# Scan steps dealt by work and tied behind a unit's matmuls, and a final norm whose sums start early

## The chip, the cores and the metric

The kernel runs on one core of a Trainium2 chip, in one launch. The metric is the device time in microseconds, median of several runs. Five instruction streams work side by side: TensorE (PE; its weight loads are PEld), VectorE (DVE), ScalarE (ACT), GpSimd (POOL) and SyncE (SP, which issues all DMAs here). Each executes its own list in order; they wait for one another through semaphores.

## The reference

One inference step of a hybrid decoder layer on 336 tokens (16 meta tokens, 256 of a prompt, 8 samples of 8). Cut to what matters here:

```python
h = rms_norm(x, norm_w)
proj = h @ w_in
z, xbc, dt_raw, sc_b, sc_c, sc_h, sc_z, g_a, g_b = split_proj(proj)
xbc_c, conv_new = causal_dwconv(xbc, conv_prev, ssd_conv_w)
xbc = jax.nn.silu(xbc_c + ssd_conv_b)
xs, bm, cm = jnp.split(xbc, [D_INNER, D_INNER + SSD_GROUPS * SSD_STATE], axis=-1)
# ssd_chunked(...), for each of 8 groups:
decay = jnp.exp(jnp.where(causal, seg, -jnp.inf))
wts = cb[..., None] * decay * dtc[:, :, None]
y_diag = jnp.einsum('bcijgr,bcjgrp->bcigrp', wts, xc)
chunk_states = jnp.einsum('bcjgr,bcjgrp,bcjgn->bcgrpn', to_end, xc, bc)
# y = y_diag + y_off; then a gated, grouped RMSNorm and a projection to D_MODEL,
# y_b = W_b(B * conv3(C * h) * silu(z_b)),
# sigmoid(g_a) * y_a + sigmoid(g_b) * y_b, the output projection, the residual, a last RMSNorm
```

## The kernel before

Channels lie on the partitions (2048 = 16 tiles of 128), tokens in the free dimension. Every product of fp32 numbers is made of three products of fp32r halves. `wblk` (L80) loads a block of 128x1024 weights (wraw, one SP DMA of 512 KB), ScalarE rounds it to whi (L84, the "hi split"), VectorE takes the rest, wlo (L86, the "lo split"). `mm` (L89) then runs 24 matmuls for a block: hi weights on hi and lo inputs (L92, L93), lo weights on hi inputs (L96). A `unit` is two such blocks into one PSUM bank "pj", of which there are two; one block of 24 matmuls is the clock of everything below. Other PSUM products use the two "ms" banks, or "yb", a tile of four banks.

First come the short conv branch and the projections around it, then eight groups of the recurrence (SSD). In group g TensorE runs four z units, then, from g = 1, the eight one-block units of `out_units(g-1)` that add the previous group's projection into ya (L646 takes two banks for each block), in groups 0 and 7 four gate units, and for g < 7 the six conv units of the next group, whose last results are BT, CT and four tiles xs: ScalarE's L394 begins a conv tile, VectorE's L396 adds the taps, L400 and L401 write xs. Between the units the 23 `yield`s of the generator `ssd(g)`, the *steps*, are dealt by `weave`. Steps named below: `rows(c)` transposes xs (L460) and BT (L462) of chunk c into two "ms" banks and multiplies BT by CT (L463); `decay(c)` is eight subtractions (L478) and an exponential (L480), for c = 1 after E = exp(W) (L476), which waits for W's broadcast load from ac_d; `state(c)` is the product L498 into an "ms" bank, copied out by L502 for c = 0; `weights(c)` multiplies (L484, L486); the samples' states are updated by L612 in two halves of two operations each, and stored (ssms). L616 and L619 spread the group norm's reciprocal root, by a diagonal and a product with ones.

The deal is by units: after unit i of n, steps run until 23 (i+1) / n are done, rounded up. The framework's scheduler then sets the order of each engine's instructions by priority and readiness in a model of time; a step may move among the splits and evacuations of the units near it.

After group 7 `out_units(7)` runs, with `merge` for the first eight tiles of ya: it loads a branch tile (mb_d) into a buffer of the tag "h0", which also holds the samples' states, and L666 and L667 write ya. The final projection has 16 units: L715 adds the residual, L717 squares, GpSimd's L719 sums the squares into sacc. The last norm (`rstd`, L114 to L125) sums over partitions by products with ones (L114, six: two tiles by three pieces of the tokens), takes the power on GpSimd (L119), and spreads the result by three diagonals (L124) and three products (L125). Sixteen scalings follow, twelve on VectorE (L729), four on ScalarE and GpSimd (L727, with the copy rsb, L735), and the stores to yT, two single tiles (L731) and seven pairs (L733).

## Time and profile before

| | us |
|---|---|
| median of three runs | 1877.46 |
| the three runs | 1880.71, 1876.68, 1877.46 |
| profiled execution | 1878.88 |
| its span | 1877.1 |
| TensorE busy | 1838.0 (98%) |
| VectorE, ScalarE, GpSimd busy | 1150.7, 752.0, 312.1 |
| mean granted TensorE clock | 0.993 of full |

A row of the timeline gives the start of an operation, its duration, engine and line, the tiles written and read, and in brackets the idle time of its engine before it with what ended that. Matmuls are pipelined, so their durations overlap and a busy TensorE isn't TensorE at its peak; a stretch is measured by its ends. The granted clock has two levels here, full (2.4 GHz) and half (1.2 GHz).

### The profile page before, as it was taken

The numbers are of one execution on the slowest core, as the hardware profiler recorded it, in microseconds if no ns is written. First come the engines' busy times: TensorE is split into PE (matmuls) and PEld (weight loads), VectorE is DVE, ScalarE is ACT, GpSimd is POOL, SyncE is SP. The second block draws the span as 40 slices with busy tenths as digits, with TensorE's granted clock in tenths as the row PEclk, the third lists the DMA queues.
The fourth block names the chain that finished last, engine by engine and source line by source line (L and its number), as shares of the span: only waits on it lengthen the run. The fifth ranks groups of instructions, "written<-read, shape, count | busy, mean of one in ns | idle before, by whom it ended". The sixth has DMA issues, their size and how long they took to land.

```text
span 1877.1 us, 31447 instructions
## 1 busy us (share of the span) xinstructions
PE 1838.0 (98%) x12622; PEld 1798.4 (96%) x12622; DVE 1150.7 (61%) x1743; ACT 752.0 (40%) x1043; POOL 312.1 (17%) x397
## 2 busy tenths in 40 slices
PE   7999999999999999999999999999999999999996
PEld 7999999999999999999999999999999999999996
DVE  6844444444534337568686776868768687674533
ACT  5433333333333335444453443534435344333432
POOL 0100000000000002131321323223232231300011
PEclk9999999999999999999999999999999999999998
DMA  6444444444444446457475564655656466575553
GB/s 219 141 153 146 147 154 149 147 148 155 150 159 156 157 159 224 154 179 241 150 235 170 184 227 157 225 170 186 217 158 228 165 200 212 169 261 169 173 171 107
DMA packets 117170, 331.74 MB, mean 177 GB/s; under 512 B 12448, under 2 KB 38688, under 8 KB 117024
## 3 DMA queue, kind: packets, MB, share of 16 engines
q1 hardware_dynamic: 117024, 329.73, 53.4%
q8 instruction: 99, 1.62, 0.3%
q14 instruction: 47, 0.39, 0.1%
HBM read 296.80 MB, written 32.88 MB: 176 GB/s over the span
## 4 chain that ended last, share of the span: by engine, by line
PE 62%; DVE 3%; DMA 2%; issue 1%; ACT 1%; POOL 0%; DVEq 0%; SPq 0%; ACTq 0%
PE pj L92 19%; PE pj L93 19%; PE pj L96 19%; PE yb L554 2%; PE ms L498 1%; DMA W<-ac_d 1%; PE ms L537 1%; DMA wraw<-w 1%; DVE cacc L396 1%; PE ms L460 1%; DVE wlo L86 1%; DVE W L478 1%; PE yb L609 0%; DVE h L612 0%; DVE ya L729 0%
## 5 line engine op out<-in xcount | busy, mean ns | idle before, releaser
L92 PE MATMUL pj<-hhi,whi 128*128 128x320 f32 (+3 forms) x2944 | 888.5, 313 | 0.0
L93 PE MATMUL pj<-hlo,whi 128*128 128x320 f32 (+3 forms) x2944 | 883.3, 312 | 0.0
L86 DVE TENSOR_TENSOR wlo<-wraw,whi 128x1024 fp32r<-128x1024 f32 x480 | 601.1, 1253 | 446.3 <-PE pj L96 283.3
L84 ACT ACTIVATE whi<-wraw 128x1024 fp32r<-128x1024 f32 x480 | 508.3, 1059 | 870.7 <-PE pj L93 801.7
L92 PEld LDWEIGHTS pj<-hhi,whi 128*128 128x128 f32 x2944 | 554.7, 188 | 4.1 <-issue 3.0
L93 PEld LDWEIGHTS pj<-hlo,whi 128*128 128x128 f32 x2944 | 553.9, 188 | 0.7
L96 PE MATMUL pj<-hhi,wlo 128*128 128x320 f32 (+3 forms) x2944 | 498.3, 311 | 0.0
L96 PEld LDWEIGHTS pj<-hhi,wlo 128*128 128x128 f32 x2944 | 453.1, 188 | 0.0
L92 PE MATMUL pj<-yh,whi 128*128 128x320 f32 x512 | 157.2, 319 | 0.0
L93 PE MATMUL pj<-yl,whi 128*128 128x320 f32 x512 | 152.3, 309 | 0.0
L92 PEld LDWEIGHTS pj<-yh,whi 128*128 128x128 f32 x512 | 96.2, 188 | 7.8 <-issue 6.7
L93 PEld LDWEIGHTS pj<-yl,whi 128*128 128x128 f32 x512 | 96.2, 188 | 1.7 <-issue 1.7
L96 PE MATMUL pj<-yh,wlo 128*128 128x320 f32 x512 | 95.8, 309 | 0.0
L396 DVE SCALAR_TENSOR_TENSOR cacc<-pad,V,cacc 128x360 f32<-128x360 f32 (+1 forms) x144 | 84.7, 588 | 9.3 <-ACT cacc L394 7.2
L646 DVE TENSOR_TENSOR ya<-ya,pj 128x320 f32<-128x320 f32 x112 | 54.4, 485 | 53.7 <-PE pj L96 52.4
L506 POOL TENSOR_TENSOR h<-h,decS 128x512 f32<-128x512 f32 x64 | 72.3, 1166 | 78.7 <-PE ms L537 78.7
L195 POOL COPY SCS<-up 128x2 f32<-128x2 f32 x16 | 19.4, 1214 | 370.9 <-DVE up L189 367.9
L96 PEld LDWEIGHTS pj<-yh,wlo 128*128 128x128 f32 x512 | 80.3, 188 | 0.0
L93 PE MATMUL pj<-vlo,whi 128*128 128x320 f32 x256 | 75.5, 309 | 0.0
L92 PE MATMUL pj<-vhi,whi 128*128 128x320 f32 x256 | 75.5, 309 | 0.0
L478 DVE TENSOR_SCALAR W<-W,act 128x128 f32<-128x128 f32 (+2 forms) x192 | 66.3, 403 | 14.6 <-DMA W<-ac_d 11.4
L389 POOL COPY pad<-cs 128x24 f32<-128x24 f32 x48 | 31.6, 661 | 130.1 <-DVE cacc L396 124.7
(211 smaller groups left out, 1483.0 us busy)
## 6 DMA issues: line engine op xcount, KB each, us to landing
wraw<-w SPq DMA_DIRECT2D x352, 512.0 KB, 3.9
wraw<-wso SPq DMA_DIRECT2D x64, 512.0 KB, 3.5
wraw<-wsc SPq DMA_DIRECT2D x32, 512.0 KB, 3.8
h<-h0T SPq DMA_DIRECT2D x32, 512.0 KB, 5.8
ssms<-h SPq DMA_DIRECT2D x32, 512.0 KB, 4.3
wraw<-wo SPq DMA_DIRECT2D x32, 512.0 KB, 3.9
xq_d<-xe SPq DMA_DIRECT2D x16, 320.0 KB, 3.4
W<-ac_d SPq DMA_DIRECT2D x8, 576.0 KB, 5.4
```

Source lines behind the costliest of these rows:

```text
L84: nc.scalar.activation(hi[:, :n], raw[:, :n], AF.Copy)
L86: nc.vector.tensor_tensor(lo[:, :n], raw[:, :n], fb(hi[:, :n]), sub)
L92: nc.tensor.matmul(out, w, xh(k0 + k), start=first and k == 0, stop=False)
L93: nc.tensor.matmul(out, w, xl(k0 + k), start=False, stop=False)
L96: nc.tensor.matmul(out, w, xh(k0 + k), start=False, stop=last and k == nk - 1)
L195: nc.gpsimd.tensor_copy(SCS[:, j, 0, :], up[:, 256:258])
L389: nc.gpsimd.tensor_copy(smp[:, :, 0:3], cs[:, 1:9, :])
L396: nc.vector.scalar_tensor_tensor(acc[:, i0:], pad[:, i0 + k:360 + k], col(V_CW, 4 * j + k), acc[:, i0:], mult, add)
L478: nc.vector.tensor_scalar(w[:n, h, :], w[:n, h, :], act[:n, c, 8 * g + h:8 * g + h + 1], 0.0, sub, ALU.min)
L506: nc.gpsimd.tensor_tensor(split(h0[b]), split(h0[b]), bc(hv(decS[:, b, :], g), [P, 8, HP]), mult)
L554: nc.tensor.matmul(yb[q * HP:(q + 1) * HP, t, t0:t0 + n], x[:, h * HP:(h + 1) * HP], w[:, h, :], start=i == 0, stop=i == 3)
L646: nc.vector.tensor_tensor(ya[:, m, :TV], ya[:, m, :TV], pp[:, :TV], add)
```

## The change

Four things change. First, `weave` counts work: a z, gate or conv unit weighs 2, an out unit 1, and after each unit as many steps run as the share of the weight passed allows, only whole ones. Second, every instruction that a step issues on TensorE, ScalarE or VectorE gets an order (not a wait on a semaphore) behind the latest L96 matmul, hi split or lo split written before it; the names are kept in `latest`. Third, E = exp(W[1]) moves from decay(1) to the step of rows(1), ahead of the loads of the samples' states. Fourth, the end: the squares of blocks 0 to 14 are summed by three products as soon as they are there, in front of the last block's end; after the last block three products, one VectorE operation, the power, one diagonal operation of 107 x 321 and one product follow; all sixteen scalings are VectorE's, and the stores go out in ten pieces.

```diff
+    latest = {}
+
     def wblk(src, n=1024):
         raw = wp.tile([P, 1024], F32, name="wraw")
         nc.sync.dma_start(raw[:, :n], src)
         hi = wp.tile([P, 1024], F32R, name="whi")
-        nc.scalar.activation(hi[:, :n], raw[:, :n], AF.Copy)
+        latest["act"] = nc.scalar.activation(hi[:, :n], raw[:, :n], AF.Copy).ins
         lo = wp.tile([P, 1024], F32R, name="wlo")
-        nc.vector.tensor_tensor(lo[:, :n], raw[:, :n], fb(hi[:, :n]), sub)
+        latest["dve"] = nc.vector.tensor_tensor(lo[:, :n], raw[:, :n], fb(hi[:, :n]), sub).ins
         return hi, lo
 
     def mm(out, hi, lo, xh, xl, base, nk, k0, first, last):
...
             w = lo[:, base + k * P:base + k * P + P]
-            nc.tensor.matmul(out, w, xh(k0 + k), start=False, stop=last and k == nk - 1)
+            latest["pe"] = nc.tensor.matmul(out, w, xh(k0 + k), start=False, stop=last and k == nk - 1).ins
...
 
             def decay(c):
                 n, m, w = CH[c][1], NT[c], W[c]
-                if c == 1:
-                    nc.scalar.activation(E, w, AF.Exp)
                 for h in range(8):
                     nc.vector.tensor_scalar(w[:n, h, :], w[:n, h, :], act[:n, c, 8 * g + h:8 * g + h + 1], 0.0,
                                             sub, ALU.min)
...
             decay(0)
             yield
+            nc.scalar.activation(E, W[1], AF.Exp)
             rows(1)
             for u in range(4):
                 h = pb.tile([P, 2, 512], F32, name="h0", bufs=4)
...
-        def weave(units, steps, lead, n):
-            done = 0
-            for i, _ in enumerate(units):
-                if i < lead:
-                    continue
-                want = (i + 1 - lead) * NSTEP / max(n - lead, 1)
-                while done < want and next(steps, "end") != "end":
+        def weave(parts, steps):
+            total, past, done = sum(n * w for _, n, w in parts), 0, 0
+            for w in (w for units, _, w in parts for _ in units):
+                past += w
+                want = NSTEP * past / total
+                traced = nc.cur_bb.bb.instructions
+                tail = traced[-1]
+                while done + 1 <= want + 1e-6 and next(steps, "end") != "end":
                     done += 1
+                new = []
+                for ins in reversed(traced):
+                    if ins is tail:
+                        break
+                    new.append(ins)
+                for ins in new:
+                    for a in latest.values():
+                        if ins.engine == a.engine:
+                            tc.add_manual_dep(ins, a.name, mybir.DependencyInfo(mybir.DependencyClass.NoSync,
+                                                                                 mybir.DependencyReason.DATA),
+                                              reason="step")
             for _ in steps:
                 pass
 
-        from itertools import chain
         S = [{} for _ in range(NG)]
         for _ in conv_units(0, S[0]):
             pass
         for g in range(NG):
-            parts = [z_units(g, S[g])]
-            n = 4
+            parts = [(z_units(g, S[g]), 4, 2)]
             if g:
-                parts.append(out_units(g - 1, S[g - 1]))
-                n += 8
+                parts.append((out_units(g - 1, S[g - 1]), 8, 1))
             if g in (0, NG - 1):
-                parts.append(gate_units(0, 4) if g == 0 else gate_units(4, 8))
-                n += 4
+                parts.append((gate_units(0, 4) if g == 0 else gate_units(4, 8), 4, 2))
             if g < NG - 1:
-                parts.append(conv_units(g + 1, S[g + 1]))
-                n += 6
-            weave(chain(*parts), ssd(g, S[g]), 0, n)
+                parts.append((conv_units(g + 1, S[g + 1]), 6, 2))
+            weave(parts, ssd(g, S[g]))
         for mp, _ in enumerate(out_units(NG - 1, S[NG - 1])):
             if mp < 4:
                 for m in (2 * mp, 2 * mp + 1):
...
-        sacc = pc_.tile([P, TV], F32, name="sacc", bufs=1)
+        sacc, sq = (pc_.tile([P, TV + 4], F32, name=n, bufs=1) for n in ("sacc", "sql"))
+        for t in (sacc, sq):
+            nc.gpsimd.memset(t[:, TV:], 0.0)
+        pr = [ps.tile([P, 512], F32, name="ms") for _ in range(2)]
+
+        def sums(i, t):
+            for c in range(3):
+                nc.tensor.matmul(pr[i][:107, c:c + 1], t[:, 107 * c:107 * c + 107], ones[:, 0:1], start=True, stop=True)
+
+        sm, r = (pc_.tile([107, 3], F32, name=n, bufs=1) for n in ("rs_m", "rs_r"))
         for m in range(KT):
             xr = pc_.tile([P, TV], F32, name="xr")
             nc.sync.dma_start(xr, xT[:, m, META:])
             po = unit(wo[m], lambda k: hhi[:, k, :TV], lambda k: hlo[:, k, :TV], TV)
             nc.vector.scalar_tensor_tensor(ya[:, m, :TV], po, 0.5, xr, mult, add)
-            sq = pc_.tile([P, TV], F32, name="sqf") if m else sacc
-            nc.scalar.activation(sq, ya[:, m, :TV], AF.Square)
-            if 0 < m < KT - 1:
-                nc.gpsimd.tensor_tensor(sacc, sacc, sq, add)
-        rs = run(rstd(pc_, [sacc, sq], META, 1.0 / DM, EPS))
-        rsb = pc_.tile([P, TV], F32, name="rsb", bufs=1)
-        for q in range(8):
-            for m in (2 * q, 2 * q + 1):
-                if q % 3 == 2:
-                    fx = pc_.tile([P, TV], F32, name="fx", bufs=4)
-                    nc.scalar.activation(fx, ya[:, m, :TV], AF.Copy, scale=col(V_FW, m))
-                    nc.gpsimd.tensor_tensor(ya[:, m, :TV], fx, rsb, mult)
-                else:
-                    nc.vector.scalar_tensor_tensor(ya[:, m, :TV], ya[:, m, :TV], col(V_FW, m), rs, mult, mult)
-                if q == 0:
-                    nc.sync.dma_start(yT[:, m, :], ya[:, m, :TV])
-            if q:
-                nc.sync.dma_start(yT[:, 2 * q:2 * q + 2, :], ya[:, 2 * q:2 * q + 2, :TV])
+            if m < KT - 1:
+                s_ = pc_.tile([P, TV], F32, name="sqf")[:, :TV] if m else sacc[:, :TV]
+                nc.scalar.activation(s_, ya[:, m, :TV], AF.Square)
+                if m:
+                    nc.gpsimd.tensor_tensor(sacc[:, :TV], sacc[:, :TV], s_, add)
+                if m == KT - 2:
+                    sums(0, sacc)
+                    nc.vector.tensor_scalar(sm, pr[0][:107, 0:3], 1.0 / DM, EPS, mult, add)
             else:
-                nc.scalar.activation(rsb, rs, AF.Copy)
+                nc.scalar.activation(sq[:, :TV], ya[:, m, :TV], AF.Square)
+        sums(1, sq)
+        nc.vector.scalar_tensor_tensor(r, pr[1][:107, 0:3], 1.0 / DM, sm, mult, add)
+        nc.gpsimd.tensor_tensor(r, r, bc(mhalf[:107], [107, 3]), ALU.pow)
+        dg = pc_.tile([107, 3, 107], F32, name="rs_d", bufs=1)
+        nc.vector.tensor_tensor(dg, bc(ident[:107, :107].unsqueeze(1), [107, 3, 107]),
+                                bc(r.unsqueeze(2), [107, 3, 107]), mult)
+        rs = ps.tile([P, 512], F32, name="pj")
+        nc.tensor.matmul(rs[:, :321], ones[:107, :], dg.rearrange("p c t -> p (c t)"), start=True, stop=True)
+        m = 0
+        for n in (1, 1, 2, 2, 2, 2, 2, 2, 1, 1):
+            for k in range(m, m + n):
+                nc.vector.scalar_tensor_tensor(ya[:, k, :TV], ya[:, k, :TV], col(V_FW, k), rs[:, :TV], mult, mult)
+            nc.sync.dma_start(yT[:, m:m + n, :], ya[:, m:m + n, :TV])
+            m += n
```

Three places in the program's order follow, the second for two engines, with the line numbers of each kernel: those of the new one are two higher in most of the code up to L476, the same from L478 to L510, and one higher from there to `merge`. In the rows, W is the exponent or weight tile of the first two chunks, W_ with a number that of the third.

VectorE at the start of a group, before; the last conv tile's xs is the fourth line from the end:

```order
L478 TENSOR_SCALAR W<-W,act 128x144 x4
L400 SCALAR_TENSOR_TENSOR xs<-cth,cacc 128x272
L401 SCALAR_TENSOR_TENSOR xs<-cth,cacc 128x64
L478 TENSOR_SCALAR W<-W,act 128x144 x4
L86 TENSOR_TENSOR wlo<-wraw,whi 128x1024
L396 SCALAR_TENSOR_TENSOR cacc<-pad_6678,V,cacc 128x360 x3
L86 TENSOR_TENSOR wlo<-wraw,whi 128x1024
L400 SCALAR_TENSOR_TENSOR xs<-cth,cacc 128x272
L401 SCALAR_TENSOR_TENSOR xs<-cth,cacc 128x64
L86 TENSOR_TENSOR wlo<-wraw,whi 128x1024
L430 SCALAR_TENSOR_TENSOR zs<-zs,pj 128x320
```

After, the same place:

```order
L88 TENSOR_TENSOR wlo<-wraw,whi 128x1024
L398 SCALAR_TENSOR_TENSOR cacc<-pad_6678,V,cacc 128x360
L478 TENSOR_SCALAR W<-W,act 128x128 x4
L402 SCALAR_TENSOR_TENSOR xs<-cth,cacc 128x272
L403 SCALAR_TENSOR_TENSOR xs<-cth,cacc 128x64
L478 TENSOR_SCALAR W<-W,act 128x128 x4
L88 TENSOR_TENSOR wlo<-wraw,whi 128x1024
L432 SCALAR_TENSOR_TENSOR zs<-zs,pj 128x320
L88 TENSOR_TENSOR wlo<-wraw,whi 128x1024
L467 TENSOR_TENSOR xdt<-ms,dtt 128x512
L88 TENSOR_TENSOR wlo<-wraw,whi 128x1024
L432 SCALAR_TENSOR_TENSOR zs<-zs,pj 128x320
```

The subtractions behind which the conv tail stood were those of decay(1) (128x144); now those of decay(0) (128x128) stand ahead of the tail and decay(1) is behind it, past the first z units.

ScalarE at the end of a group's z units, before; L429 takes a z bank, L502 copies state(0) out:

```order
L467 ACTIVATE bt<-ms 128x128
L84 ACTIVATE whi<-wraw 128x1024 x2
L429 ACTIVATE zs<-pj 128x320
L502 ACTIVATE hst<-ms 128x512
L84 ACTIVATE whi<-wraw 128x1024
L467 ACTIVATE bt<-ms 80x128
L568 ACTIVATE bhh<-bt 80x128
```

After:

```order
L86 ACTIVATE whi<-wraw 128x1024 x2
L431 ACTIVATE zs<-pj 128x320
L86 ACTIVATE whi<-wraw 128x1024
L480 ACTIVATE W_10905<-W_10905 80x640
L502 ACTIVATE hst<-ms 128x512
L469 ACTIVATE bt<-ms 80x128
L86 ACTIVATE whi<-wraw 128x1024 x6
```

The exponential of the third chunk (80x640) now stands directly ahead of L502, where it followed later, beyond the rows shown, before.

TensorE at the first out unit of a group, before; yh and yl are inputs of out_units, L498 is state(0), L460 to L463 are rows(2):

```order
L498 MATMUL ms<-xe,bt 128x512
L92 MATMUL pj<-yh,whi 128x320
L93 MATMUL pj<-yl,whi 128x320
L92 MATMUL pj<-yh,whi 128x320
L93 MATMUL pj<-yl,whi 128x320
L92 MATMUL pj<-yh,whi 128x320
L93 MATMUL pj<-yl,whi 128x320
L92 MATMUL pj<-yh,whi 128x320
L93 MATMUL pj<-yl,whi 128x320
L96 MATMUL pj<-yh,wlo 128x320 x4
L460 MATMUL ms<-CR,xs 80x128 x4
L462 MATMUL ms<-CR,BT 80x128
```

After; L462 to L465 are rows(2):

```order
L98 MATMUL pj<-yh,wlo 128x320 x4
L498 MATMUL ms<-xe,bt 128x512
L462 MATMUL ms<-CR,xs 80x128 x4
L94 MATMUL pj<-yh,whi 128x320
L95 MATMUL pj<-yl,whi 128x320
L94 MATMUL pj<-yh,whi 128x320
L464 MATMUL ms<-CR,BT 80x128
L465 MATMUL ms<-CT,BT 80x80
L95 MATMUL pj<-yl,whi 128x320
```

The state product and the rows of chunk 2, a block's part apart before, now follow one another, and the BT transpose comes a few matmuls behind.

VectorE at the start of out_units(7), with buffer numbers, before; L612 updates the samples' states, L666 and L667 are merge:

```order
L612 TENSOR_TENSOR h0_16027<-h0_16027,yb_16746 128x1024
L612 TENSOR_TENSOR h0_16029<-h0_16029,yb_16746 128x1024
L86 TENSOR_TENSOR wlo_16869<-wraw_16865,whi_16867 128x1024
L86 TENSOR_TENSOR wlo_16915<-wraw_16911,whi_16913 128x1024
L646 TENSOR_TENSOR ya_79<-ya_79,pj_16825 128x320
L666 SCALAR_TENSOR_TENSOR zs_16853<-zs_16853,ya_79 128x320
L667 TENSOR_TENSOR ya_79<-zs_16853,h0_16855 128x320
L646 TENSOR_TENSOR ya_79<-ya_79,pj_16839 128x320
L86 TENSOR_TENSOR wlo_16961<-wraw_16957,whi_16959 128x1024
L666 SCALAR_TENSOR_TENSOR zs_16859<-zs_16859,ya_79 128x320
```

After:

```order
L613 TENSOR_TENSOR h0_16028<-h0_16028,yb_16810 128x1024
L613 TENSOR_TENSOR h0_16030<-h0_16030,yb_16810 128x1024
L647 TENSOR_TENSOR ya_79<-ya_79,pj_16825 128x320
L667 SCALAR_TENSOR_TENSOR zs_16853<-zs_16853,ya_79 128x320
L647 TENSOR_TENSOR ya_79<-ya_79,pj_16839 128x320
L668 TENSOR_TENSOR ya_79<-zs_16853,h0_16855 128x320
L667 SCALAR_TENSOR_TENSOR zs_16859<-zs_16859,ya_79 128x320
L88 TENSOR_TENSOR wlo_16961<-wraw_16957,whi_16959 128x1024
L668 TENSOR_TENSOR ya_79<-zs_16859,h0_16861 128x320
L647 TENSOR_TENSOR ya_79<-ya_79,pj_16871 128x320
L667 SCALAR_TENSOR_TENSOR zs_16899<-zs_16899,ya_79 128x320
```

The second update moved to directly ahead of the first merge, behind two more lo splits.

## Rows read from the trace of the kernel before

**Rows 1.** The page, part 1: busy time of each engine, share of the span, instructions.
```profile
PE 1838.0 (98%) x12622; PEld 1798.4 (96%) x12622; DVE 1150.7 (61%) x1743; ACT 752.0 (40%) x1043; POOL 312.1 (17%) x397
```

**Rows 2.** TensorE's waits: engine, line, releaser: us in total, times, longest.
```profile
PE ms L460 <- DVE xs L400: 13.2, 7, 3.4
```

**Rows 3.** Timeline, TensorE: start, us, line, operation [idle before, releaser].
```profile
1338.78 0.33 PE L460 MATMUL ms<-CR,xs 128*128 128x128 f32 x1 [3.40 <-DVE xs L400]
```

**Rows 4.** Windows: us; busy PE, PEld, DVE, ACT, POOL; PEclk, DMA share, GB/s.
```profile
1339.40:1343.00 3.60, 3.60 (x16) 3.60 (x15) 3.57 (x5) 0.28 (x1) 1.04 (x1) 0.53 1.01 384
...
1661.00:1679.00 18.00, 18.00 (x123) 17.75 (x121) 16.50 (x30) 5.43 (x7) 0.00 (x0) 1.00 0.85 272
1870.00:1874.00 4.00, 0.00 (x0) 0.00 (x0) 1.31 (x3) 0.00 (x0) 0.00 (x0) 0.50 1.04 363
```

**Rows 5.** Timeline, ScalarE and VectorE, around a group's start.
```profile
1094.69 1.17 ACT L476 ACTIVATE E<-W 128x1152 f32<-128x1152 f32 x1 [1.56 <-DMA W<-ac_d]
...
1100.73 1.17 ACT L480 ACTIVATE W<-W 128x1152 f32<-128x1152 f32 x1 [3.13 <-DVE W L478]
1101.81 0.67 ACT L394 ACTIVATE cacc<-pad,V 128x360 f32<-128x360 f32 x1
...
1105.42 0.44 DVE L400 SCALAR_TENSOR_TENSOR xs<-cth,cacc 128x272 f32<-128x272 f32 x1
```

**Rows 6.** Timeline, all engines, end of the program.
```profile
1852.09 0.30 PE L92 MATMUL pj<-hhi,whi 128*128 128x320 f32 x1
...
1853.49 0.88 POOL L719 TENSOR_TENSOR sacc<-sacc,sqf 128x320 f32<-128x320 f32 x1 [5.91 <-ACT sqf L717]
...
1860.47 0.36 PE L114 MATMUL ms<-CR,sqf 128*112 128x1 f32 x2 [1.04 <-ACT sqf L717]
...
1861.65 0.16 DVE L118 TENSOR_SCALAR rs_m<-ms 112x3 f32<-112x3 f32 x1 [1.79 <-PE ms L114]
...
1862.79 0.47 DVE L124 TENSOR_SCALAR rs_d<-CR,rs_r 112x112 f32<-112x112 f32 x2 [0.97 <-POOL rs_r L119]
...
1865.07 1.01 DVE L729 SCALAR_TENSOR_TENSOR ya<-ya,V,ms 128x320 f32<-128x320 f32 x2 [0.86 <-PE ms L125]
...
1866.64 4.67 DVE L729 SCALAR_TENSOR_TENSOR ya<-ya,V,ms 128x320 f32<-128x320 f32 x10 [0.56 <-ACT rsb L735]
...
1868.38 4.88 SPq L733 DMA_DIRECT2D yT<-ya  x7
```

**Rows 7.** Timeline, TensorE and ScalarE, end of group 0's z units.
```profile
781.85 1.02 PE L498 MATMUL ms<-xe,bt 128*128 128x512 f32 x2
...
782.90 0.60 ACT L502 ACTIVATE hst<-ms 128x512 f32<-128x512 f32 x1 [0.42 <-PE ms L498]
...
783.55 0.31 PE L462 MATMUL ms<-CR,BT 128*80 128x128 f32 x1
```

**Rows 8.** Groups by line and shape: count | busy us, mean ns | idle before, releaser.
```profile
L86 DVE TENSOR_TENSOR wlo<-wraw,whi 128x1024 fp32r<-128x1024 f32 x480 | 601.1, 1253 | 446.3 <-PE pj L96 283.3 <-ACT whi L84 161.9
...
L612 DVE TENSOR_TENSOR h<-h,yb 128x1024 f32<-128x1024 f32 x32 | 38.7, 1215 | 0.0
...
L478 DVE TENSOR_SCALAR W<-W,act 80x80 f32<-80x80 f32 x64 | 22.2, 406 | 0.5 <-DMA W<-ac_d 0.5
...
L619 PE MATMUL ms<-xe,CR 107*128 107x321 f32 x16 | 6.2, 472 | 0.0
...
L480 ACT ACTIVATE W<-W 80x640 f32<-80x640 f32 x8 | 5.9, 740 | 5.3 <-DVE W L478 5.3
```

**Rows 9.** Timeline, VectorE, one group's decay(2).
```profile
1167.64 1.90 DVE L478 TENSOR_SCALAR W<-W,act 80x80 f32<-80x80 f32 x7
```

**Rows 10.** DMA issues: line or tiles, count, KB each, median us from issue to landing.
```profile
ssms<-h SPq DMA_DIRECT2D x32, 512.0 KB, 4.3
...
h<-mb_d SPq DMA_DIRECT2D x16, 160.0 KB, 3.6
...
yT<-ya SPq DMA_DIRECT2D x2, 160.0 KB, 1.8
```


## The prediction

> **What bounds the kernel now.** I read the engine totals first, then TensorE's waits, then the stretches around the longest of them. TensorE is at work for 1838.0 of 1877.1 us [rows 1]; VectorE, ScalarE and GpSimd have room on average. So only three things can be won: time in which TensorE waits, time in which its clock is at half, and the head and tail, where it has nothing to do. The list of waits names one repeated case: rows(c)'s first transpose (L460) waits for the conv output xs (L400), 13.2 us in seven times, the longest 3.4 [rows 2]. Each is at the start of a group; the longest ends at 1338.78 [rows 3], and the six others are 13.2 - 3.4 = 9.8 together, 1.6 each. After the 3.40 us one the granted clock is 0.53 of full (the 1.2 GHz level) for 3.60 us, where work that takes half as long at full speed was done [rows 4]; at full speed this stretch would have been worth 3.60 x 0.53 = 1.9 us. That wait therefore costs another 1.7. After the six shorter ones no such drop is recorded.
>
> Why xs is late is in ScalarE's and VectorE's rows of another group, an ordinary one [rows 5]. E = exp(W[1]) waits 1.56 for a DMA; the eight subtractions of decay(1) (L478) come behind it; the exponential of W (L480) at 1100.73 waits 3.13 for them; and L394, the first operation of the *last conv tile*, stands behind L480 in ScalarE's queue at 1101.81. Its tail, L400, runs at 1105.42 + 0.44 = 1105.86, over 11 us after E began. A step of the recurrence with a slow input thus stands ahead of the conv tail on two queues, and rows(0) asks for this tail right away.
>
> The last matmuls of the final projection end near 1859.2, and from there the tail is serial: sums, reciprocal root, spread, scaling, stores, to 1877.1 [rows 6].
>
> **The change, part by part.** The sum is made against the profiled execution, 1878.88 us (span 1877.1), which is 1.42 above the median of 1877.46.
>
> *1. rows(0) later, decay(1) and E behind the conv tail: -13.2 and -1.7.* Step by work, rows(0) is dealt two blocks of weights later, one z unit. TensorE does 123 matmuls in 18.00 us [rows 4], 0.146 each, so a block of 24 takes 3.51 and rows(0) comes 7.0 later. The decay and E, which delayed xs, now stand behind L400 in both queues. To bring the wait back, xs would have to be later than today by 7.0 - 3.4 = 3.6 even in the worst group. I take the whole 13.2 and the 1.7 of clock (the lower bound, half of it, is a rival below).
>
> *2. A new wait, rows(2): +3.2 (0 to 11).* state(0) and rows(2) were about one block apart and now meet in one. The two "ms" banks are then held by state(0)'s product, which ScalarE's L502 must copy out, and by the L460 transposes, so the BT transpose (L462 before, L464 after) waits for L502. The trace of before has this meeting once, ahead of the first out units: L498 starts at 781.85, L502 at 782.90 for 0.60, L462 at 783.55 [rows 7]. From this row: L498 and the four L460 take 0.85 and 0.36, so TensorE comes to the BT transpose 3.51 + 0.85 + 0.36 + 3 x 0.146 = 5.2 after the out unit begins. New is that L502 stands behind L480 of the third chunk (0.740), and this behind eight 80x80 subtractions of decay(2), which share VectorE with a lo split (1.253) [rows 8], z's product (L430) and one evacuation, both 128x320 as the final scalings and taken as these, 4.67 / 10 = 0.47 [rows 6]. Seven of the eight took 1.90 in one run [rows 9], 0.27 each; their mean over the program is 0.406 [rows 8]. At 0.27: 1.25 + 0.47 + 0.27 + 0.47 + 1.90 = 4.4, plus 0.74, 0.60 and 0.1 for hand-overs = 5.8, a wait of 0.6; if the split was already done, the evacuation starts when twelve matmuls are through (1.76): 1.76 + 0.47 + 1.90 + 1.44 = 5.6, a wait of 0.4; if W's decay was early, none. At 0.406: 1.25 + 0.47 + 0.47 + 8 x 0.406 + 1.44 = 6.9 by the same chain, rounded down to a wait of 1.4 since TensorE may do two more matmuls first. I take 0.4 for each of eight groups, 3.2, as the run of seven is nearest: GpSimd, whose work may slow VectorE's, waits for L502 itself then. Behind L502 in ScalarE's queue stand the copy of bt and the next hi split; behind the waiting transpose stand the out unit's matmuls.
>
> *3. z's last bank: +0.5 (0 to 2).* The out unit's second product takes the bank of the last z unit at 1.76, and L430, which frees it, ends at 1.25 + 0.47 = 1.72 if the split is ahead of it: a tie, 0 to 0.25 in eight groups.
>
> *4. Around the last group: +2.5 (0.9 to 4.5).* The second state update (L612, two of 1.215 [rows 8]) moves from ahead of out_units(7)'s stretch to its first blocks. VectorE is busy there for 16.50 of 18.00 us [rows 4]; 16.50 + 2.43 = 18.93, so 0.9 over, the low end. The merge's loads of mb_d for its third and fourth tile also reuse the h0 buffers of that update: they come only after its stores (4.3 to landing) and take 3.6 themselves [rows 10]. 2.43 + 4.3 + 3.6 = 10.3 after the update begins, against 7.0 (two blocks) until the first tile of that pair is wanted: 3.3 late, of which VectorE, on whose queue the next evacuations stand behind the merge, lets through what two free "pj" banks don't cover (one half unit, 1.76): 1.6. Together 0.9 + 1.6 = 2.5; the high end, 0.9 + 3.6, has the whole delay and a little issue time.
>
> *5. Early sums: +1.4 (0.7 to 1.6).* Three column sums of the first fifteen blocks now stand inside block fifteen's first half, at 1852.09 + 11 x 0.146 = 1853.7, and want GpSimd's last addition, which ends at 1853.49 + 0.88 = 1854.37 [rows 6]: a wait of 0.7. Six such sums went from 1860.47 to 1861.65 and took 1.18, so three take 0.59; a switch of operands is 0.1.
>
> *6. The tail: -2.5 (-3.6 to -1.2).* Three sums fewer at the end: -0.59. Diagonal and spread took from 1862.79 to the first scaling at 1865.07, 2.28. Now one VectorE operation (0.47 for two of the old three blocks [rows 6], so 0.5 to 0.7) and one 321-column product (0.472 per pass at full clock, two passes, so 0.94 [rows 8]; up to 1.9 at half clock) follow: about 1.6, -0.7. Then the stores. Before: the scalings start at S = 1865.07, ScalarE's copy costs VectorE a wait of 0.56, GpSimd holds back the first pair, the last store's issue ends at 1868.38 + 4.88 = 1873.26, and the program ends 3.8 later, S + 12.0. After: sixteen scalings of 0.467 are 7.5, an issue 0.35, and then 2.1 to 3.8 for a smaller last store: S + 9.9 to 11.7, I take 10.8, -1.2. The stores ran at 363 GB/s [rows 4], so 2.6 MB need 7.2 us and are not slower than the scalings. -0.59 - 0.7 - 1.2 = -2.5.
>
> The last 320 KB store becomes two of 160 KB. Two such stores landed 1.8 us after issue [rows 10]. The Trainium skill, "DMA: Bandwidth & Descriptors", section "Bandwidth", asks for batches of 1 MiB or more and puts a 64 KB transfer at 138 GB/s, a 1 MB one at 341; by it the split speaks against the change. At the lower of these rates a 160 KB store would take 1.2 us, an estimate from that page, where 363 GB/s give 0.45, so the two would cost 1.5 more at the end and the sum would be 1869.2 and not 1867.7. The row of 1.8 includes all of it, and the sum goes by the row.
>
> *7. Other moves: 0 +/- 1.* Steps are dealt elsewhere, with about as many switches of operands as before; the same operations are executed. Each step tied behind the latest split can come at most one block later, and nothing but TensorE is full.
>
> Sum: -13.2 - 1.7 + 3.2 + 0.5 + 2.5 + 1.4 - 2.5 = -9.8. 1878.88 - 9.8 = 1869.1; less 1.4 to the median: 1867.7, said as 1868. With all low ends: -14.9 + 0.9 + 0.7 - 3.6 = -16.9, 1860.6; with all high ends: -14.9 + 11 + 2 + 4.5 + 1.6 - 1.2 = +3.0, 1880.5.
>
> **The rivals.** *No new waits* (L502 in time, merge loads early): the low ends, about 1862. For it: in the one meeting of before the wait was 0.2 us. Against: L480 was not ahead of L502 there.
>
> *Half the gain*: the xs wait stays in some groups, because a lo split or the conv of the tile before it, not decay(1), was the last thing behind L400 (L400 began 3.6 after L394 did) [rows 5]. Half of 14.9 is 7.4: 1875 less the smaller stalls that it hides, about 1874.
>
> *No change*: the BT transpose's wait is 1.6 per group, 12.9 in eight, 9.7 more than taken: 1877.
>
> *Slower*: the same wait on the far side. With decay(2) at 0.406 and a second lo split (1.25) ahead of it on VectorE, it is 1.4 + 1.25 = 2.65 per group, 21.2 in all, 18 more than taken: 1886. The point from which it decides is 1.6 per group for no gain and 2.1 for a loss that shows. Against: the new order has one split there, not two, and the tie holds decay(2) behind that one alone.
>
> *The steps don't move* (the ties change no queue): the order of the new kernel shows that they do, so no chance of its own.
>
> **How the numbers follow.** Forecast 1868 (1864.5 to 1872): 0.64. No new waits, 1862: 0.13. Half the gain, 1874: 0.09. No change, 1877: 0.07. Slower, 1886: 0.07. This measurement can tell about 0.2% (3.75 us), so faster means below 1873.7, slower above 1881.2. The first two and most of the third (0.07) are faster: 0.84; the rest of it and the fourth are the same: 0.09; slower 0.07. The range leaves out the ends: the lowest part of "no new waits" and everything above half the gain: 1861.5 to 1874.
>
> **What would show it.** Right: no L460 wait on xs in TensorE's list, clock 1.00 through 1339 to 1343, a new wait of some tenths of the BT transpose on ScalarE's L502 in each group, one wait near 1850 for GpSimd's sum, and a tail from the last matmul some 2.5 shorter. Wrong: waits on xs that persist (step 1), a BT wait above 1.5 (step 2), a half clock after it, evacuations in out_units(7) late by over 4 (step 4), or a tail as long as before (step 6).

## The result, and the profile after

The changed kernel takes 1869.97 us (median of five runs, 1868.78 to 1870.82) where the one before takes 1877.46: a ratio of 0.9948, interval 0.9929 to 0.9968. The forecast was 1868. A gain of 7.5 us was measured, 9.5 had been forecast. The profiled span is 1868.7 against 1877.1.

In the profile after, TensorE's list of waits (engine, line, releaser: us in total, times, longest) has no xs in it; these rows take the place of [rows 2]:

```profile
PE pj L176 <- ACT whi L86: 9.1, 1, 9.1
PE pj L94 <- DVE zs L432: 2.5, 3, 1.4
...
PE pj L750 <- DVE rs_d L747: 1.7, 1, 1.7
PE pj L94 <- DVE ya L647: 1.6, 2, 1.0
PE ms L464 <- ACT hst L502: 1.6, 1, 1.6
PE ms L725 <- ACT sql L742: 1.1, 1, 1.1
PE ms L725 <- POOL sacc L737: 0.8, 1, 0.8
```

The first is the start of the program, as before. New in the recurrence are z's last bank (L432), rows(2)'s transpose (L464) behind L502 and evacuations (L647); new at the end is the early sums' wait for GpSimd (L737). Engine totals, and the granted clock (seventh number of the window's row, after the five busy times) at the place of the half-speed stretch of [rows 4]:

```profile
PE 1836.0 (98%) x12618; PEld 1792.8 (96%) x12618; DVE 1122.9 (60%) x1746; ACT 748.8 (40%) x1038; POOL 299.5 (16%) x395
```

```profile
1337.00:1341.00 4.00, 4.00 (x31) 3.99 (x30) 0.82 (x2) 0.02 (x1) 3.66 (x2) 1.00 0.84 302
```

Where the 8.3 us of span (unrounded) went I read by laying the starts of the same block in both traces side by side, from block 8 on, where both are past the first norm. The new kernel is ahead by 0.9 at block 8, by 9.8 when group 7 comes to its last two gate units, by 7.9 after out_units(7), by 6.3 after the early sums, and by 8.3 at the end. So: start +0.9, groups +8.9, the last two gate units and out_units(7) -1.9, early sums -1.7, tail +2.1.

z's last bank: TensorE's wait in group 1, and then a timeline of all engines in an ordinary group:

```profile
898.03 0.41 PE L94 MATMUL pj<-yh,whi 128*128 128x320 f32 x1 [1.37 <-DVE zs L432]
```

```profile
1121.78 1.04 POOL L486 TENSOR_TENSOR xe<-xdt,tet 128x512 f32<-128x512 f32 x1 [9.61 <-DVE xdt L467]
1121.97 1.93 DVE L88 TENSOR_TENSOR wlo<-wraw,whi 128x1024 fp32r<-128x1024 f32 x1
...
1123.83 1.34 DVE L484 TENSOR_TENSOR W<-W,cbm 128x1152 f32<-128x1152 f32 x1
...
1125.10 1.21 DVE L88 TENSOR_TENSOR wlo<-wraw,whi 128x1024 fp32r<-128x1024 f32 x1
1126.23 0.47 DVE L432 SCALAR_TENSOR_TENSOR zs<-zs,pj 128x320 f32<-128x320 f32 x1
...
1127.20 1.28 DVE L478 TENSOR_SCALAR W<-W,act 80x80 f32<-80x80 f32 x7
...
1129.19 0.72 ACT L480 ACTIVATE W<-W 80x640 f32<-80x640 f32 x1
...
1129.82 0.58 ACT L502 ACTIVATE hst<-ms 128x512 f32<-128x512 f32 x1
1130.45 0.31 PE L464 MATMUL ms<-CR,BT 128*80 128x128 f32 x1
```

A split of 1.93 (beside GpSimd's L486; 1.21 without), L484 and another split run without a gap, and the z product that frees the bank comes behind them. L502 ends at 1130.40 and the BT transpose starts at 1130.45, without a wait. In the last group, where state(0) comes one block earlier, it does wait, for the chain that the prediction named:

```profile
1583.12 0.74 ACT L480 ACTIVATE W<-W 80x640 f32<-80x640 f32 x1 [1.64 <-DVE W L478]
1583.76 0.41 ACT L431 ACTIVATE zs<-pj 128x320 f32<-128x320 f32 x1
1584.08 0.58 ACT L502 ACTIVATE hst<-ms 128x512 f32<-128x512 f32 x1
...
1584.71 0.31 PE L464 MATMUL ms<-CR,BT 128*80 128x128 f32 x1 [1.62 <-ACT hst L502]
```

At out_units(7) VectorE waits for the merge's load, and TensorE 3 us later for an evacuation behind it; ahead of this stretch it waits for another one (timelines of VectorE and of TensorE):

```profile
1660.81 0.49 DVE L668 TENSOR_TENSOR ya<-zs,h 128x320 f32<-128x320 f32 x1 [0.89 <-DMA h<-mb_d]
```

```profile
1606.12 0.39 PE L94 MATMUL pj<-yh,whi 128*128 128x320 f32 x1 [0.70 <-DVE ya L647]
...
1663.79 0.38 PE L94 MATMUL pj<-yh,whi 128*128 128x320 f32 x1 [0.95 <-DVE ya L647]
```

The end, to be laid beside [rows 6]:

```profile
1846.79 0.72 PE L725 MATMUL ms<-CR,sacc 128*107 128x1 f32 x6 [0.84 <-POOL sacc L737]
...
1854.12 0.72 PE L725 MATMUL ms<-CR,sql 128*107 128x1 f32 x6 [1.08 <-ACT sql L742]
1854.88 0.16 DVE L744 SCALAR_TENSOR_TENSOR rs_r<-ms,rs_m 107x3 f32<-107x3 f32 x1 [1.32 <-PE ms L725]
...
1856.01 0.49 DVE L747 TENSOR_TENSOR rs_d<-CR,rs_r 107x321 f32<-107x321 f32 x1 [0.97 <-POOL rs_r L745]
1856.56 1.31 PE L750 MATMUL pj<-rs_d,CR 107*128 107x321 f32 x2 [1.72 <-DVE rs_d L747]
1857.91 7.42 DVE L754 SCALAR_TENSOR_TENSOR ya<-ya,V,pj 128x320 f32<-128x320 f32 x16 [1.40 <-PE pj L750]
1858.48 7.36 SPq L755 DMA_DIRECT2D yT<-ya  x10
```

The scalings start at S = 1857.91 and the program ends at 1868.7, S + 10.8.

### The profile page after: what moved, and what is told of

Read it like the earlier page. It is cut to its first block, busy times and chain, and to the rows that moved or that the text cites. A ratio compares the mean times of both kernels' runs of the same rounds, so it can differ in the third digit from the quotient of the medians.

```text
span 1868.7 us, 31432 instructions
## 1 busy us (share of the span) xinstructions
PE 1836.0 (98%) x12618; PEld 1792.8 (96%) x12618; DVE 1122.9 (60%) x1746; ACT 748.8 (40%) x1038; POOL 299.5 (16%) x395
## 4 chain that ended last, share of the span: by engine, by line
PE 49%; DVE 1%; issue 1%; DMA 0%; ACT 0%; POOLq 0%; POOL 0%; DVEq 0%; ACTq 0%
PE pj L94 15%; PE pj L95 15%; PE pj L98 15%; PE yb L555 1%; PE ms L498 1%; PE ms L538 1%; DVE wlo L88 0%; PE ms L462 0%; DVE ya L754 0%; PE yb L610 0%; PE ms L559 0%; PE ms L465 0%; PE ms L620 0%; DMA wraw<-wso 0%; PE ms L599 0%
## 5 line engine op out<-in xcount | busy, mean ns | idle before, releaser
L398 DVE SCALAR_TENSOR_TENSOR cacc<-pad,V,cacc 128x360 f32<-128x360 f32 (+1 forms) x144 | 89.6, 622 | 2.8
L647 DVE TENSOR_TENSOR ya<-ya,pj 128x320 f32<-128x320 f32 x112 | 54.1, 485 | 60.0 <-PE pj L98 59.5
L392 POOL COPY cs<-pad 128x3 f32<-128x3 f32 x48 | 42.4, 884 | 124.4 <-ACT pad L389 124.4
L95 PEld LDWEIGHTS pj<-vlo,whi 128*128 128x128 f32 x256 | 48.1, 188 | 0.0
```

The source lines that it names most:

```text
L95: nc.tensor.matmul(out, w, xl(k0 + k), start=False, stop=False)
L392: nc.gpsimd.tensor_copy(cs[:, 0, :], pad[:, 272:275])
L398: nc.vector.scalar_tensor_tensor(acc[:, i0:], pad[:, i0 + k:360 + k], col(V_CW, 4 * j + k), acc[:, i0:], mult, add)
L647: nc.vector.tensor_tensor(ya[:, m, :TV], ya[:, m, :TV], pp[:, :TV], add)
```

## The experiments

My theory was that dealing rows(0) two blocks later takes the xs waits away, and that the new waits come from VectorE's queue between the last conv tile and the first out unit. The rivals: the ties do it, E's place alone does it, or the gain is the end's. All ratios are to the kernel before, run beside each kernel. The column "from block 8" is the gain of the profiled span over that of the kernel before, less what stood at block 8, where executions of one kernel already differ (below). It holds some 1.7 of the half-speed stretch of [rows 4], which is in the profile of the kernel before; behind block 8 and ahead of the tail, e8 and e7 have one such stretch of their own, e4 has five, and the other profiles of the table none.

| kernel | listed waits on xs, z's bank | ratio (interval) | from block 8 |
|---|---|---|---|
| changed | 0, 2.5 | 0.9948 (0.9929 to 0.9968) | 7.4 |
| changed, again | 0, 0.4 | 0.9936 (0.9917 to 0.9955) | 9.6 |
| e1, end only | 12.9, 0 | 0.9992 (0.9977 to 1.0007) | 2.5 |
| e8, before with E moved | 14.7, 0 | 1.0005 (0.9994 to 1.0016) | -1.4 |
| e2, no ties | 0, 0 | 0.9904 (0.9883 to 0.9925) | 15.9 |
| e3, old deal with ties | 0, 0 | 0.9916 (0.9895 to 0.9937) | 14.4 |
| e4, E back | 0, 13.9 | 1.0078 (1.0056 to 1.0101) | -14.4 |
| e10, no ties, E back | 0, 0 | 0.9910 (0.9891 to 0.9928) | 14.5 |
| e12, no ties on VectorE | 0, 0 | 0.9920 (0.9902 to 0.9939) | 11.9 |
| e7, steps behind z's product | 0, 0.6 | 0.9969 (0.9956 to 0.9981) | 5.7 |
| e5, sums later | 0, 3.7 | 0.9944 (0.9930 to 0.9957) | 7.9 |
| e6, other merge buffers | 0, 2.2 | 0.9945 (0.9932 to 0.9958) | 8.2 |
| e9, no ties, three mends | 0, 0 | 0.9897 (0.9877 to 0.9918) | 16.1 |

**The end alone.** The kernel before with the new code from sacc on.

```diff
-        rs = run(rstd(pc_, [sacc, sq], META, 1.0 / DM, EPS))
...
+        sums(1, sq)
...
+        nc.tensor.matmul(rs[:, :321], ones[:107, :], dg.rearrange("p c t -> p (c t)"), start=True, stop=True)
...
```

> The kernel before with only the new end (early sums, one spreading product, VectorE scalings, ten stores). Theory (the gain is the removed waits on xs in the groups): the tail after the last residual addition gets 2.1 us shorter, as in the changed kernel (17.74 to 15.63), the early sums cost 1.6 on TensorE in the last block, so the whole is 0.5 faster, 1877.0 against 1877.5, and the seven xs waits of 13.2 us stay in TensorE's list. Rival (the end carries the gain): 1872 or less.

Measured 1879.32 beside 1880.32, ratio 0.9992. TensorE's list keeps the xs waits:

```profile
PE ms L460 <- DVE xs L400: 12.9, 7, 2.5
```

So the gain isn't the end's, whose 2.0 here are for the most part used up by the early sums' 1.4. The longest xs wait here is 2.5 us, and the granted clock stays full behind all seven: the 3.40 of [rows 3] and what it cost are not in every execution.

**E alone.** The kernel before, with E moved as in the change.

```diff
-                if c == 1:
-                    nc.scalar.activation(E, w, AF.Exp)
...
+            nc.scalar.activation(E, W[1], AF.Exp)
             rows(1)
```

> The kernel before with only E's move to the step of rows(1). Theory: VectorE's decay(1) no longer waits for E, but ScalarE's exponential of W stays ahead of the last conv tile; the xs waits shrink by the 0 to 1 us that E cost in each group: 6 to 13 us remain, 1870 to 1877. Rival (E alone delays the conv tail): the waits go, 1864.

Measured 1879.38 beside 1879.57, with the waits a little longer:

```profile
PE ms L460 <- DVE xs L400: 14.7, 7, 3.2
```

E's place doesn't remove them; even the small gain that I expected wasn't there. The granted clock is at half beside one of these waits, of 2.31 us, but not behind the longest, of 3.20 (windows at the end of each wait):

```profile
989.72:993.13 3.41, 3.10 (x13) 3.10 (x14) 3.38 (x7) 0.85 (x3) 0.81 (x1) 0.50 0.88 311
1455.79:1459.00 3.21, 3.21 (x23) 3.21 (x24) 3.18 (x6) 0.70 (x3) 0.92 (x1) 1.00 0.99 341
```

**No ties.** The changed kernel without the dependencies.

```diff
-                for ins in new:
-                    for a in latest.values():
-                        if ins.engine == a.engine:
-                            tc.add_manual_dep(ins, a.name, mybir.DependencyInfo(mybir.DependencyClass.NoSync,
...
```

> The changed kernel without the orders behind the latest matmul and splits; the deal by work stays, so rows(0) still stands two blocks later on TensorE. Theory (the later rows(0) removes the waits): no xs wait, 1868 to 1871. Rival (the ties hold decay(1) behind the conv tail, and this removes the waits): the subtractions come ahead of the tail again, xs waits of 6 us or more in all, 1876 or more.

Measured 1862.04 beside 1880.32: no xs wait, as the theory has it, but faster than it allowed. Of the list after, these are all that remain in the groups and the last block:

```profile
PE ms L712 <- POOL sacc L724: 0.8, 1, 0.8
...
PE pj L94 <- DVE ya L647: 0.5, 1, 0.5
```

The later rows(0) is enough (E is early here too; e10 below does without that), and in this deal the ties cost 6 to 8 us on top. VectorE's timelines of one group show what a tie does. Without ties, decay(1) (L478, 128x144) runs among the last conv tile's operations, part of it ahead of xs (L402):

```profile
1098.26 3.23 DVE L478 TENSOR_SCALAR W<-W,act 128x144 f32<-128x144 f32 x3 [3.29 <-ACT E L513]
1101.41 0.43 DVE L402 SCALAR_TENSOR_TENSOR xs<-cth,cacc 128x272 f32<-128x272 f32 x1
...
1103.84 0.69 DVE L478 TENSOR_SCALAR W<-W,act 128x144 f32<-128x144 f32 x3
```

In the changed kernel all eight come after two z units, ahead of weights(1) and decay(2), in the stretch where z's banks must be freed. That decay(1) stands ahead of xs does no harm without ties, since TensorE asks for xs later still. The first row is the changed kernel's, of VectorE, the second TensorE's without ties:

```profile
1117.85 1.72 DVE L478 TENSOR_SCALAR W<-W,act 128x144 f32<-128x144 f32 x8
```

```profile
1103.33 0.60 PE L462 MATMUL ms<-CR,xs 128*128 128x128 f32 x4
```

**Old deal, ties kept.**

```diff
-            total, past, done = sum(n * w for _, n, w in parts), 0, 0
+            total, past, done = sum(n for _, n, w in parts), 0, 0
...
-                past += w
+                past += 1
...
-                while done + 1 <= want + 1e-6 and next(steps, "end") != "end":
+                while done < want and next(steps, "end") != "end":
```

> The changed kernel with the old deal (equal share for each unit, rounded up), ties kept: rows(0) stands after the first z unit again, decay(0) and decay(1) stay behind the conv tail on VectorE. Theory: xs waits come back, shorter, since no decay stands ahead of the tail: 3 to 10 us in all, 1873 to 1878. Rival (the ties alone are enough): no xs waits, within 1 us of the changed kernel's 1870.

Measured 1863.90 beside 1880.32, no xs wait at all, and some 6 us faster than the rival allowed. My theory falls in so far as it took the later rows(0) for the one cause: rows(0) stands where it stood before, in the second block of the z units, xs (L402) is written at 1096.31 + 0.43, and the transposes start at 1098.45 without a wait:

```profile
1096.31 0.43 DVE L402 SCALAR_TENSOR_TENSOR xs<-cth,cacc 128x272 f32<-128x272 f32 x1
1096.80 1.65 DVE L478 TENSOR_SCALAR W<-W,act 128x128 f32<-128x128 f32 x8
...
1098.45 0.60 PE L462 MATMUL ms<-CR,xs 128*128 128x128 f32 x4
```

The tie holds even decay(0) behind xs. Either edit alone removes the waits, at 0.9904 and 0.9916; both together took 0.9936 to 0.9948.

**E back in decay(1),** everything else as changed, and then the same without ties.

```diff
+                if c == 1:
+                    nc.scalar.activation(E, w, AF.Exp)
...
-            nc.scalar.activation(E, W[1], AF.Exp)
             rows(1)
```

> The changed kernel with E = exp(W[1]) back in decay(1); all else stays. Theory: E has no part in the gain once decay(1) is behind the conv tail, within 1 us of the changed kernel. Rival (E's early place spares VectorE a wait at decay(1)): ScalarE does E and the exponential of W in a row, z's last bank is freed about 1 us later in groups 1 to 7, 1875.

> No ties, deal by work, and E = exp(W[1]) back in decay(1). Theory (E's place matters only where the ties hold decay(1) behind it late in the z units): no waits on xs or z's bank above 0.5 us in a group, within 3 us of the version without ties, 0.990 to 0.992 of the kernel before. Rival (E in front of decay(1) costs VectorE its wait in any deal): waits on z's bank of 1 us or more in most groups, 1.0 or above, as with the ties.

With ties 1892.95 beside 1880.32, slower than before; without ties 1863.42 beside 1881.17, as without ties at all. TensorE's list of the first:

```profile
PE pj L94 <- DVE zs L432: 13.9, 6, 2.7
```

The rows name another reason than the one I gave (ScalarE). Groups by line and shape, of this kernel, and then of the changed one, name the multiplication of the first chunk in weights(0) (columns: us in all, mean ns):

```profile
L486 DVE TENSOR_TENSOR W<-W,cbm 128x1024 f32<-128x1024 f32 x8 | 27.1, 3384 | 0.0
```

```profile
L484 DVE TENSOR_TENSOR W<-W,cbm 128x1024 f32<-128x1024 f32 x8 | 9.8, 1220 | 0.0
```

The same operation takes 3.38 us in the mean instead of 1.22. The timeline of GpSimd and VectorE in one group of it shows beside what:

```profile
1122.05 2.95 POOL L490 TENSOR_TENSOR E<-E,CT 128x1152 f32<-128x1152 f32 x1 [4.66 <-ACT E L478]
```

```profile
1122.39 3.69 DVE L486 TENSOR_TENSOR W<-W,cbm 128x1024 f32<-128x1024 f32 x1
```

With E late, GpSimd's product of E and CT starts 0.34 us ahead of VectorE's multiplication, which then ends 1.1 us after GpSimd's does, about the time that it takes by itself: as if it began to move when GpSimd was done. Early, as in the change, GpSimd does it some 8 us ahead of that multiplication, and VectorE, which waits 3.98 us for the next hi split, has nothing to do in half of that time:

```profile
1108.50 2.67 POOL L488 TENSOR_TENSOR E<-E,CT 128x1152 f32<-128x1152 f32 x1 [7.86 <-ACT E L513]
```

```profile
1113.84 1.23 DVE L88 TENSOR_TENSOR wlo<-wraw,whi 128x1024 fp32r<-128x1024 f32 x1 [3.98 <-ACT whi L86]
```

The Trainium skill, "SBUF — State Buffer", section "Who interferes with whom", states this rule: a VectorE instruction with two inputs in SBUF and a GpSimd instruction that reads SBUF exclude one another, and whoever comes second waits. The numbers here agree, 3.69 being near 2.95 - 0.34 + 1.22 = 3.8.

The clock is the other part of this loss. Beside five of this kernel's seven waits for z's bank and L502 the granted clock is at half, for 20.5 us together; one such stretch:

```profile
1134.57:1137.98 3.41, 3.07 (x11) 3.07 (x12) 2.05 (x10) 0.53 (x1) 0.00 (x0) 0.50 0.60 190
```

At full clock TensorE does a block's matmul in 0.146 us, 23 in that time, so half of the 20.5 is lost, about 10 by this estimate. Longer waits on z's bank and L502 (17.9 against 4.1) are 13.8. The two make up the 21.8 from block 8 that lie between this kernel and the changed one, to some 2 us.

**Ties on TensorE and ScalarE alone.**

```diff
-                        if ins.engine == a.engine:
+                        if ins.engine == a.engine and a is not latest["dve"]:
```

> The changed kernel with the ties on TensorE and ScalarE alone, none on VectorE. Theory (VectorE's ties push decay(1), weights(1) and decay(2) past the conv tail into the z units, where they stand ahead of z's product): z's bank wait and the last group's wait for L502 go, 0.990 to 0.992 of the kernel before, as without any tie. Rival (ScalarE's ties, which hold L480 ahead of L502 and E late): waits of 4 us or more stay, 0.994 to 0.996.

Measured 1865.14 beside 1881.17, and neither z's bank nor L502 stands in TensorE's list. So those waits are, in this deal, the doing of VectorE's ties, which cost 2.3 to 4.5 us by the column from block 8 (11.9 against 9.6 and 7.4). They are not all that the ties cost: against no ties at all 4.0 are still missing. By the starts of the blocks 2.6 of these are lost at the place of state(0), 0.43 in each of six groups: the ties on TensorE put rows(2) directly behind it, and in group 1 the next matmul starts 0.86 after the first of L498, where without ties it is a block's matmul, 0.46 after. 0.9 falls in the last group, where a wait of 0.70 for an evacuation (L647) stays, and 0.4 in the tail, where the spreading product took 1.26 at a granted clock of 0.58 instead of 0.81 at full clock.

**Steps behind z's product too.**

```diff
-                nc.vector.scalar_tensor_tensor(z[:, :TV], z[:, :TV], 1.0, pz, add, mult)
+                latest["dve"] = nc.vector.scalar_tensor_tensor(z[:, :TV], z[:, :TV], 1.0, pz, add, mult).ins
```

> The changed kernel, with VectorE's steps tied behind z's product, which frees z's bank, too. Theory (TensorE's waits for z's last bank, 3.2 us in four groups beyond the pace, come from weights(1) and splits ahead of that product on VectorE): they go, and rows(2)'s transpose waits instead, since the eight subtractions of decay(2) and their exponential come later: 0 to 1.5 in each of eight groups; together 1867 to 1873. Rival (the wait for the bank is for the lo split, not the steps): the 2.5 us of listed waits stay, 1870.

Measured 1873.21 beside 1879.57. TensorE's list has what the theory says, z's bank nearly gone and the wait for L502 grown, in the last group:

```profile
PE ms L464 <- ACT hst L502: 3.4, 1, 3.4
...
PE pj L94 <- DVE zs L432: 0.6, 2, 0.3
```

What one wait gave up, 1.9, came back in the other, 1.8. Behind the 3.39 us wait the granted clock is at half (0.50 from 1586.26 to 1589.68), which costs another 1.7, and from block 8 this kernel is 1.7 behind the changed one. The total is just above what I gave (1867 to 1873).

**Early sums later.** Three products behind the first half of the last unit.

```diff
...
+            if half == 0 and mid:
+                mid()
...
```

> The changed kernel with the three early sums behind the last block unit's first half instead of inside it. Theory (the sums cost a wait of 0.84 for GpSimd's addition, 0.72 of products and a switch): the wait goes, 0.8 faster than the changed kernel, 1869.2 against 1870. Rival (the wait is hidden by the weights' arrival anyway): no difference.

Measured 1867.49 beside 1879.57 (0.9944; the changed kernel 0.9936 to 0.9948): not to be told apart by the times. Its profile is of the slowest of its six executions, 1872.07, with 3.7 for z's bank. By the block starts the sums cost 0.5 instead of 1.7, and GpSimd is no longer in the list: in their own stage the theory holds, and the wait wasn't hidden.

**Other buffers for the merge.**

```diff
-            mt = pb.tile([P, 2, 512], F32, name="h0", bufs=4)[:, 0, :TV]
+            mt = big("hst", 2)[:, :TV] if m in (2, 3) else pb.tile([P, 2, 512], F32, name="h0", bufs=4)[:, 0, :TV]
```

> The changed kernel; in the merge, the branch tiles of the third and fourth tile go into buffers that held the carried state (free by then) instead of those of the samples' second update. Theory (VectorE's wait for that load, 0.9 us, passes a wait of 0.95 on to TensorE at out_units(7)): both waits go, 1.0 to 1.1 faster, 1869. Rival (VectorE is full there, with the second update moved into the stretch): the load is there, TensorE still waits 0.5 to 1.0, no difference.

Measured 1869.47 beside 1879.57. VectorE's wait for the load goes, TensorE's wait of 0.95 becomes 0.41, and its loss over the last two gate units and out_units(7) falls by the block starts from 1.9 to 1.3. So about a third of it was the load. That the rest is the full VectorE is argued, not shown; the theory and the rival each have a part.

**No ties, sums later, another deal in the last group.**

```diff
...
-                parts.append((out_units(g - 1, S[g - 1]), 8, 1))
+                parts.append((out_units(g - 1, S[g - 1]), 8, 1 if g < NG - 1 else 1.5))
...
-                parts.append((gate_units(0, 4) if g == 0 else gate_units(4, 8), 4, 2))
+                parts.append((gate_units(0, 4) if g == 0 else gate_units(4, 8), 4, 2 if g == 0 else 1))
...
```

> The deal by work without ties, the early sums behind the last block's first half, and in the last group weights 1.5 for out units and 1 for gate units, so that the second state update comes one unit before out_units(7). Theory: against the version without ties, 0.8 less for the sums, 0.9 less at out_units(7) and 0.6 less before it: 0.989 of the kernel before, 8 to 13 us faster than the changed kernel. Rival (what a stall there gives up comes back in the next wait): no faster than without ties, 0.9904.

Measured 1861.47 beside 1881.17, 0.9897, with the changed kernel at 1868.01 on the same chip: faster than both kernels, by 19.7 and 6.5 us, where I expected 8 to 13 for the second. Against no ties alone (0.9904) the intervals overlap. By the block starts out_units(7) loses 1.2 less and the sums 1.2 less than without ties alone, but from block 8 only 0.3 is left of that: the last group lost 0.8 ahead of out_units(7), where I expected a gain of 0.6, the other groups lost 0.5, and from the diagonal to the first scaling it took 2.03 against 1.40, with TensorE's product at half clock (0.50 against 1.00). So the rival isn't excluded.

## Why the prediction was right, point by point

- **Step 1, waits on xs and the clock: -13.2 and -1.7.** Of the first nothing is left in any profile of the changed kernel. The cause given, one step ahead of the conv tail on two queues with rows(0) asking right away, is right too, but I took both edits for needed: e2 and e3 show that each is enough. The clock's 1.7 is the weak part. Of the three profiles with the xs waits, that of the kernel before and e8's have one stretch at half clock (e8's beside a wait of 2.31, with none behind its 3.20) and e1's has none, so it belongs to an execution and not to every run. Taken from the profile's own time and then again less 1.4 to the median, it was probably counted twice; 1869.1 would have been nearer, but that is argued, not shown.
- **Step 2, rows(2) behind L502: +3.2 (0 to 11).** The mechanism is there, the count isn't: 1.6 in the last group, none in the seven others, where the subtractions took 0.18 each, less than the lower row of 0.27, and were through before L498.
- **Step 3, z's last bank: +0.5 (0 to 2).** The mis-sized term: 2.5 listed in one profile, 0.4 in another, 3.7 in e5. I counted one split ahead of z's product and left out what stood ahead of that split in VectorE's queue, weights(1) and a split slowed by GpSimd. e12 shows that VectorE's ties put it there.
- **Step 4, the merge: +2.5.** 1.9 by the block starts, with the load's wait of 0.89 that was named; e6 takes 0.65 of it away with the load. A wait of 0.70 at 1606.12 on an evacuation was not foreseen.
- **Step 5, early sums: +1.4.** 1.6 to 1.7: wait 0.84 for 0.7, products 0.72 for 0.59.
- **Step 6, the tail: -2.5.** -2.1. The stores came as worked out, S + 10.8. The sums gave 0.4 (0.76 against 1.18), diagonal and spread 0.4 (1.90 against 2.28) where 0.7 was taken; the product took 1.31 at a granted clock of 0.58 over its stretch, inside the bounds that I gave. The ten stores cost nothing that the rows show. By the estimate from the Trainium skill, "DMA: Bandwidth & Descriptors", section "Bandwidth", they would have cost 1.5 more, S + 12.3; the rows don't agree with it, and the page's figure is for loads issued by GpSimd, where these are stores issued by SP.
- **Step 7, other moves: 0 +/- 1.** What is left of the sum: -13.2 - 1.7 + 1.6 + 2.5 + 1.9 + 0.7 + 1.7 - 2.1 = -8.6, with 0.9 of the start -9.5, against 8.3 measured: 1.2 is missing. One term of this step can be named. The changed kernel has the same meeting of state(0) and rows(2) as e12, and laid beside e2 its six middle groups lose 2.4 more than the listed waits. So another 1.2 must have been won elsewhere; where is not known.

That the total came within 2 us of the forecast is partly luck: step 2 was 1.6 too high and step 3 2.0 too low, and the 0.9 of the start and the 2.4 of step 7 stand in no term.

None of the rivals came. The one that was worth having, that the change contains an edit that costs (the ties, 6 to 8 us), was not among them: I wrote that a tied step "can come at most one block later, and nothing but TensorE is full", and that sentence is what failed. VectorE is at 60% over the program, but in the group shown above, from the third z unit to the first out unit (1113.84 to 1128.48), it worked 14.58 of 14.64 us, after an idle 3.98. And the ties had a price on TensorE too, the 2.4 to 2.6 at state(0), which lies in the order and not in a full queue.

## What to carry to other kernels

Where a wait can be removed from either side, the asker later or the producer earlier, do one and measure before doing the other: here both together pushed the same work into a stretch that had no room. An order that keeps helper work behind the main engine's next operand is not free; ask what it pushes that work in front of. And ask of an operation moved on GpSimd what VectorE does beside it.

## What the runs showed of the hardware that was not expected

Two profiled executions of the changed kernel are 2.5 us apart at the start of block 8 already (60.44 and 57.93). Its second set of runs shows 1866.2 three times and 1869.9 three times; whether that is the same difference is not shown. Windows after the first norm of its two profiles, the first at 1870.82 and the second at 1866.19, show the granted clock (after the five busy times) at half in one and full in the other, with the same code and a stall of the same kind ahead of it (TensorE waited 1.85 and 1.00 us for the sum of squares; e12 waited 0.66 and ran at half from 38.25 to 41.66, e3 waited 1.03 and kept full clock):

```profile
41.50:44.00 2.50, 2.50 (x11) 2.50 (x11) 2.23 (x4) 0.52 (x2) 0.00 (x0) 0.50 0.01 2
```

```profile
41.50:44.00 2.50, 2.50 (x19) 2.50 (x18) 2.50 (x7) 1.43 (x3) 0.00 (x0) 1.00 0.36 98
```

Later in the program it is alike: the clock fell to half beside waits of 2.31 (e8) and 3.39 us (e7), and stayed full behind 2.49 (e1) and 3.20 (e8). The length of a wait alone doesn't tell which. Whole times of this kernel should therefore be compared by several runs, and stages by their own starts.
